# Weight pieces with both halves in one tile, the stationary ones 64 bytes behind its beginning

## The chip, the core and the metric

The kernel runs on one NeuronCore of a Trainium2 chip. The core has a matrix engine (TensorE, in the profile PE for its matmuls and PEld for its loads of the stationary operand), a vector engine (VectorE, DVE), a scalar engine (ScalarE, ACT), GpSimd (POOL) and a queue engine (SyncE, SP), which issues nearly all DMAs here. The metric is the time of one execution on the device, in microseconds (us); less is better. Matmuls write to PSUM; everything else lies in SBUF, 128 partitions wide.

A matmul has two operands in SBUF. The stationary one (128 partitions x 128 columns) is loaded into the array first, by an instruction of its own (LDWEIGHTS); the moving one (here 256 or 512 columns) is then streamed past it.

## The reference

Two layers work on x of 256 positions x 1024 features, float32. Each layer is three sublayers; each sublayer normalizes its input (RMS), computes, normalizes the result and adds it to x:

```python
for i in range(DEPTH):                     # DEPTH = 2
    h = swiglu(rms_norm(x, g[0]), w_gate[i,0], w_up[i,0], w_down[i,0]);  x = x + 0.5*rms_norm(h, g[1])
    m = dilated_attention(...) if i == 0 else retention(...);            x = x + rms_norm(m, g[3])
    h = swiglu(rms_norm(x, g[4]), w_gate[i,1], w_up[i,1], w_down[i,1]);  x = x + 0.5*rms_norm(h, g[5])
# swiglu(h) = (silu(h @ w_gate) * (h @ w_up)) @ w_down;  w_gate, w_up: 1024 x 2816, w_down: 2816 x 1024
# dilated_attention: h @ w_in (1024 x 9216: q, k, v of three groups), banded softmax, @ w_out (1024 x 1024)
# retention: h @ w_in (1024 x 8192: q, k, v, two gates), two scans, gates, @ w_out (2048 x 1024)
```

So there are four SwiGLU sublayers (FFNs), one attention and one retention, and every weight is used once.

## The kernel before

**Three products for one.** Every product of activations with weights is made of three matmuls in the type fp32r: each operand is split into a high half (a copy rounded to fp32r) and a low half (what is left), and high x high, high x low and low x high are summed in PSUM (`mm3`, L183 to 188, and the three calls of `unit_t`, L375 to 377).

**The stream of weights** (class `Stream`). A list, written down before anything runs, holds all weights in the order of use. A group is 1 MB; SP loads it into one of two `raw` buffers. A group has two pieces of [128, 1024], that is, two row blocks of 128 rows by 512 columns. `split` (L94 to 120) makes the halves of a piece: ACT writes `whi` (L109 or, where a norm's gain is multiplied in, L115, twice 512 columns), DVE then writes `wlo` (L110 or L116). `whi` and `wlo` are two tags of a pool with six buffers each, so the split runs up to six pieces ahead of the matmuls. The first pieces of a sublayer can also go to buffers that are free just then; these tiles (`wx`) hold both halves in one tile already. When the matmuls of a piece are written down, `done` calls `refill`, which writes down the split of the piece six places ahead. A `raw` buffer comes free with the split of its second piece, and the next load is issued then.

**Two ways to use a piece.** In the natural form (`piece`, `unit`, `down`: lines L186 to 188 of the profile) a block of the activations (`xh`, `xl`, `hh`, `hl` and the like, 128 columns) is stationary and 512 columns of the piece move; a piece has 2 row blocks x 2 tiles of positions x 3 = 12 such matmuls. In the transposed form (`unit_t`, L375 to 377) 128 columns of the piece are stationary and the 256 positions of `xh` or `xl` move; a piece has 2 row blocks x 4 column blocks x 3 = 24 such matmuls. For one block of columns the order is `whi` with `xh`, `whi` with `xl`, `wlo` with `xh`. An FFN has 11 units of four pieces before its down product: the first two are natural, the other nine (u = 2 to 10, `ffn_t`) transposed. In the attention the first unit and the six v units are natural, the other eleven q and k units transposed. Retention and all down products are natural.

**Places.** `xh` and `xl` have rows of 320 elements per row block (1280 bytes), and a block of 128 columns of a piece is 512 bytes, so that within their tiles all these operands begin at multiples of 256 bytes. `rows` (L383 to 393) makes a [128, 256] table, `rowsf` in an FFN, `rowsq` and `rowsk` in the attention, each in a buffer of its own; a transposed FFN unit multiplies its gate by `rowsf` (L344).

Of the kernel before, what the change touches and what calls it, by code (L numbers as in the profile page):

```python
# [6 lines left out]
F32 = mybir.dt.float32  # L7
F32R = mybir.dt.float32r
# [6 lines left out]
P = 128  # L15
# [3 lines left out]
EPS = 1e-6  # L19
NK = D // P  # L20
XC = 2 * P + 64
BIG = 1.0e30
NEWTON = -8192.0
WARM = 8
# [2 lines left out]
class Stream:  # L27


    def __init__(self, K, raw_bufs, ring):  # L30
        self.K = K
        self.raw_bufs, self.ring = raw_bufs, ring
        self.groups = []
        self.pieces = []
        self.raw = {}
        self.tiles = {}
        self.n_dma = 0
        self.n_split = 0
        self.extra = {}

    def spare(self, pieces, tags):

        self.extra.update(zip(pieces, tags))

    def add_rows(self, srcs, rows, norm):

        first = len(self.pieces)
        for k0 in range(0, rows, 4):
            g = len(self.groups)
            self.groups.append(("rows", srcs, k0))  # L50
            for j in range(2):
                k = k0 + 2 * j
                self.pieces.append((g, j, None if norm is None else norm * NK + k))
        return list(range(first, len(self.pieces)))

    def add_down(self, src, rows):

        first = len(self.pieces)
        for k0 in range(0, rows, 2):
            g = len(self.groups)  # L60
            self.groups.append(("down", src, k0))
            for j in range(2):
                self.pieces.append((g, j, None))
        return list(range(first, len(self.pieces)))
# [27 lines left out]
    def split(self):  # L92
        if self.n_split >= len(self.pieces):
            return  # L94
        i = self.n_split
        self.n_split += 1
        g, j, gain = self.pieces[i]
        while self.n_dma <= g:
            self.dma()
        nc = self.K.nc  # L100
        raw = self.raw[g][:, j * 1024 : (j + 1) * 1024]
        if i in self.extra:
            both = self.K.sb.tile([P, 2, 1024], F32R, tag=self.extra[i], name=f"wx{i}")
            hi, lo = both[:, 0], both[:, 1]
        else:
            hi = self.K.sb.tile([P, 1024], F32R, tag="whi", bufs=self.ring, name=f"whi{i}")
            lo = self.K.sb.tile([P, 1024], F32R, tag="wlo", bufs=self.ring, name=f"wlo{i}")
        if gain is None:
            nc.scalar.activation(hi, raw, AF.Copy)  # L109
            nc.vector.tensor_tensor(out=lo, in0=raw, in1=hi.bitcast(F32), op=ALU.subtract)  # L110
        else:
            for kk in range(2):
                s = slice(kk * 512, kk * 512 + 512)
                gc = self.K.gcol[:, gain + kk : gain + kk + 1]
                nc.scalar.activation(hi[:, s], raw[:, s], AF.Copy, scale=gc)  # L115
                nc.vector.scalar_tensor_tensor(  # L116
                    out=lo[:, s], in0=raw[:, s], scalar=gc, in1=hi[:, s].bitcast(F32),
                    op0=ALU.mult, op1=ALU.subtract,
                )
        self.tiles[i] = (hi, lo)  # L120
        if j == 1:
            del self.raw[g]
            while self.n_dma < len(self.groups) and self.n_dma <= g + self.raw_bufs:
                self.dma()
# [16 lines left out]
class Trunk:  # L141
# [93 lines left out]
    def pre_alloc(self, name):  # L235
        self.xh = self.sb.tile([P, NK, XC], F32R, tag="xh", name=f"xh_{name}")
        self.xl = self.sb.tile([P, NK, XC], F32R, tag="xl", name=f"xl_{name}")
        self.rstd = self.sm.tile([P, 2], F32, tag="rstd", bufs=2, name=f"rstd_{name}")
# [66 lines left out]
    def plan_ffn(self, l, i):  # L305
        wg, wu, wd = self.ffn_w_gate[l, i], self.ffn_w_up[l, i], self.ffn_w_down[l, i]
        n = l * 6 + (0 if i == 0 else 4)
        units = []
        for c in range(5):
            s = slice(c * 512, c * 512 + 512)  # L310
            units.append(self.ws.add_rows([wg[:, s]], NK, n))
            units.append(self.ws.add_rows([wu[:, s]], NK, n))
        units.append(self.ws.add_rows([wg[:, 2560:], wu[:, 2560:]], NK, n))
        return dict(units=units, down=self.ws.add_down(wd, DFF // P), l=l, n=n)

    def piece(self, j, pc, accs, ts, cols=(0, P)):
# [66 lines left out]
    def rows(self, cols, name):  # L383

        nc, sb = self.nc, self.sb
        d = sb.tile([P, 2, P], F32, tag="dg", name=f"dg_{name}")
        for t in range(2):
            nc.vector.tensor_scalar(out=d[:, t, :], in0=self.ident, scalar1=cols[:, t : t + 1], scalar2=None, op0=ALU.mult)
        tr = self.trb(f"rw_{name}")
        nc.tensor.matmul(tr[:, : 2 * P], self.ones, d, start=True, stop=True)  # L390
        r = sb.tile([P, 2 * P], F32, tag=f"rows{name}", name=f"rows{name}")
        nc.vector.tensor_copy(r, tr[:, : 2 * P])
        return r

# [152 lines left out]
    def plan_attn(self, l, j):  # L547
        units = []
        for o in range(2):
            for kind, g in (("q", 0), ("k", 0), ("q", 1), ("k", 1), ("q", 2), ("k", 2), ("v", 0), ("v", 1), ("v", 2)):  # L550
                c = g * 3072 + "qkv".index(kind) * D + o * 512
                units.append((o, kind, g, self.ws.add_rows([self.attn_w_in[j, :, c : c + 512]], NK, l * 6 + 2)))
        return dict(units=units, out=self.ws.add_down(self.attn_w_out[j], NK), l=l)

    def bias_inputs(self):
# [7 lines left out]
    def bias_table(self):  # L563
# [6 lines left out]
        rt = sb.tile([33, 48], F32, tag="E1", name="rt")  # L570
        nc.vector.memset(rt, BIG)
        nc.vector.tensor_scalar(out=rt[:32, :], in0=tr[:32, :48], scalar1=-1.0, scalar2=None, op0=ALU.mult)
# [479 lines left out]
```

## Time and profile before

| | |
|---|---|
| median of 3 runs | 1310.99 us (1310.36 to 1311.44) |
| the profiled execution | 1309.44 us |
| its span, first to last instruction | 1307.6 us, granted clock 0.997 |
| moved by DMA | 235.72 MB, mean 180 GB/s |

The profile is of one execution. It lists the busy time of each engine, the chain of work that ended last, and the groups of instructions by source line with the mean duration of one. Matmuls overlap in the pipeline, so the recorded duration of one (283 ns for 256 columns) is longer than the distance between two starts; what a matmul costs is read from how many start in a stretch of time.

### The profile page before, as it was taken

To read this page: it belongs to the slowest core of one execution; us is meant where nothing else is said; L and a number is where in the kernel's file an instruction comes from. 1 tells how busy PE (TensorE), PEld (TensorE's weight loads), DVE (VectorE), ACT (ScalarE), POOL (GpSimd) and SP (SyncE) were. 2 spreads that over 40 slices of the span, in tenths; PEclk is the share of its full clock that TensorE was granted. 3 is DMA by queue.
4 is the path that set the end of the run, shared out by engine and by line. 5 is a ranking of instruction groups with operands and counts; after the bars stand their busy time and mean duration, and the time that the engine had idled before them with its cause. 6 is when DMAs were issued, how large, how long until landed. Compare 5 with 4: busy or idle time off the path is not lost.

```text
span 1307.6 us, 20776 instructions
## 1 busy us (share of the span) xinstructions
PE 1289.3 (99%) x8362; PEld 1148.9 (88%) x8362; DVE 893.0 (68%) x1593; ACT 695.9 (53%) x1073; POOL 19.8 (2%) x17
## 2 busy tenths in 40 slices
PE   8999999999999999999999999999999999999997
PEld 6999988987998779999889998877888888899986
DVE  5766547668567768866477665589887875766644
ACT  4645445456445557854455554455555545555442
POOL 1000001000000000000000000000000000000000
PEclk9999999999999999999999999999999999999999
DMA  7655556764664346555546555645554655555551
GB/s 215 226 169 189 193 195 187 207 218 138 185 210 162 129 150 223 190 174 192 193 148 224 193 173 183 211 149 171 161 172 152 180 173 193 169 196 171 190 194 64
DMA packets 130092, 235.72 MB, mean 180 GB/s; under 512 B 25403, under 2 KB 42283, under 8 KB 129996
## 3 DMA queue, kind: packets, MB, share of 16 engines
q1 hardware_dynamic: 129852, 234.14, 56.1%
q8 instruction: 65, 1.06, 0.3%
q14 instruction: 31, 0.25, 0.1%
q10 hardware_dynamic: 144, 0.26, 0.1%
HBM read 232.21 MB, written 1.12 MB: 178 GB/s over the span
## 4 chain that ended last, share of the span: by engine, by line
PE 90%; DVE 4%; DMA 2%; ACT 2%; issue 1%; SPq 0%; DVEq 0%; ACTq 0%
PE ac_f L375 11%; PE ac_f L377 11%; PE ac_f L376 11%; PE d_f L187 6%; PE d_f L186 6%; PE d_f L188 6%; PE rt L188 4%; PE rt L187 4%; PE rt L186 4%; PE at L376 3%; PE at L377 3%; PE at L375 3%; PE at L186 2%; PE at L188 2%; PE at L187 2%; PE ac_f L186 1%
## 5 line engine op out<-in xcount | busy, mean ns | idle before, releaser
L115 ACT ACTIVATE whi<-raw,gcol 128x512 fp32r<-128x512 f32 x596 | 394.0, 715 | 321.1 <-PE ac_f L376 103.9
L116 DVE SCALAR_TENSOR_TENSOR wlo<-raw,gcol,whi 128x512 fp32r<-128x512 f32 x596 | 417.5, 748 | 157.9 <-ACT whi L115 157.1
L110 DVE TENSOR_TENSOR wlo<-raw,whi 128x1024 fp32r<-128x1024 f32 x112 | 137.2, 1225 | 136.4 <-ACT whi L109 136.1
L109 ACT ACTIVATE whi<-raw 128x1024 fp32r<-128x1024 f32 x112 | 118.8, 1061 | 169.1 <-PE d_f L188 98.5
L186 PE MATMUL d_f<-whi,hhf 128*128 128x512 f32 x352 | 137.2, 390 | 0.0
L187 PE MATMUL d_f<-wlo,hhf 128*128 128x512 f32 x352 | 137.0, 389 | 0.0
L188 PE MATMUL d_f<-whi,hlf 128*128 128x512 f32 x352 | 137.0, 389 | 0.0
L376 PE MATMUL at<-xl_f,whi 128*128 128x256 f32 x352 | 99.7, 283 | 0.0
L375 PE MATMUL at<-xh_f,whi 128*128 128x256 f32 x352 | 99.7, 284 | 0.0
L377 PE MATMUL at<-xh_f,wlo 128*128 128x256 f32 x352 | 99.6, 283 | 0.0
L186 PE MATMUL rt<-whi,xh_f 128*128 128x512 f32 x244 | 95.6, 392 | 0.2 <-ACT xh_f L232 0.2
L187 PE MATMUL rt<-wlo,xh_f 128*128 128x512 f32 x244 | 95.8, 392 | 0.0
L188 PE MATMUL rt<-whi,xl_f 128*128 128x512 f32 x244 | 95.1, 390 | 0.0
L375 PE MATMUL ac_f<-xh_in,whi 128*128 128x256 f32 x288 | 81.8, 284 | 0.0
L376 PE MATMUL ac_f<-xl_in,whi 128*128 128x256 f32 x288 | 81.6, 283 | 0.0
L377 PE MATMUL ac_f<-xh_in,wlo 128*128 128x256 f32 x288 | 81.6, 283 | 0.0
L375 PE MATMUL ac_f<-xh_at,whi 128*128 128x256 f32 x288 | 81.6, 283 | 0.0
L375 PE MATMUL ac_f<-xh_rt,whi 128*128 128x256 f32 x288 | 81.6, 283 | 0.0
L375 PE MATMUL ac_f<-xh_f,whi 128*128 128x256 f32 x288 | 81.6, 283 | 0.0
L377 PE MATMUL ac_f<-xh_at,wlo 128*128 128x256 f32 x288 | 81.5, 283 | 0.0
L377 PE MATMUL ac_f<-xh_rt,wlo 128*128 128x256 f32 x288 | 81.5, 283 | 0.0
L376 PE MATMUL ac_f<-xl_rt,whi 128*128 128x256 f32 x288 | 81.5, 283 | 0.0
(346 smaller groups left out, 2855.2 us busy)
## 6 DMA issues: line engine op xcount, KB each, us to landing
raw<-in_ffn_w_down_dram SPq DMA_DIRECT2D x44, 1024.0 KB, 4.8
raw<-in_ffn_w_up_dram SPq DMA_DIRECT2D x40, 1024.0 KB, 5.0
raw<-in_ffn_w_gate_dram SPq DMA_DIRECT2D x39, 1024.0 KB, 5.0
raw<-in_attn_w_in_dram SPq DMA_DIRECT2D x36, 1024.0 KB, 5.1
raw<-in_ret_w_in_dram SPq DMA_DIRECT2D x24, 1024.0 KB, 5.7
raw<-in_ret_w_in_dram SPq DMA_DIRECT2D x16, 512.0 KB, 3.9
raw<-in_ret_w_out_dram SPq DMA_DIRECT2D x8, 1024.0 KB, 4.8
raw<-in_ffn_w_gate_dram SPq DMA_DIRECT2D x10, 512.0 KB, 4.2
```

Of the source, the lines that this page charges most:

```text
L109: nc.scalar.activation(hi, raw, AF.Copy)
L110: nc.vector.tensor_tensor(out=lo, in0=raw, in1=hi.bitcast(F32), op=ALU.subtract)
L115: nc.scalar.activation(hi[:, s], raw[:, s], AF.Copy, scale=gc)
L116: nc.vector.scalar_tensor_tensor(out=lo[:, s], in0=raw[:, s], scalar=gc, in1=hi[:, s].bitcast(F32), op0=ALU.mult, op1=ALU.subtract,)
L186: mm(out, xh, wh, start=start, stop=False)
L187: mm(out, xh, wl, start=False, stop=False)
L188: mm(out, xl, wh, start=False, stop=stop)
L375: mm(out, hi[:, s], xh, start=k == 0 and a == 0, stop=False, skip_group_check=True)
L376: mm(out, hi[:, s], xl, start=False, stop=False, skip_group_check=True)
L377: mm(out, lo[:, s], xh, start=False, stop=k == NK - 1, skip_group_check=True)
```

## The change

The two halves of a piece become one tile `w` of 2 x 1024 + 64 elements, six buffers. A set `still` holds the pieces that will be used by `unit_t`; in these the high half begins 16 elements (64 bytes) behind the beginning of the tile and the low half right behind it; in all others at the beginning itself. The tiles of `extra` stay as they are. The ring grows from 6 x 8192 to 6 x 8448 bytes of each partition; to make room `rowsf` takes the buffer of `rowsq`.

```diff
+WC = 2 * 1024 + 64
...
-    def add_rows(self, srcs, rows, norm):
+    def add_rows(self, srcs, rows, norm, still=False):
...
+        if still:
+            self.still.update(range(first, len(self.pieces)))
...
-            hi = self.K.sb.tile([P, 1024], F32R, tag="whi", bufs=self.ring, name=f"whi{i}")
-            lo = self.K.sb.tile([P, 1024], F32R, tag="wlo", bufs=self.ring, name=f"wlo{i}")
+
+            both = self.K.sb.tile([P, WC], F32R, tag="w", bufs=self.ring, name=f"w{i}")
+            o = 16 if i in self.still else 0
+            hi, lo = (both[:, z : z + 1024] for z in (o, o + 1024))
...
-            units.append(self.ws.add_rows([wg[:, s]], NK, n))
-            units.append(self.ws.add_rows([wu[:, s]], NK, n))
-        units.append(self.ws.add_rows([wg[:, 2560:], wu[:, 2560:]], NK, n))
+            units.append(self.ws.add_rows([wg[:, s]], NK, n, c > 0))
+            units.append(self.ws.add_rows([wu[:, s]], NK, n, c > 0))
+        units.append(self.ws.add_rows([wg[:, 2560:], wu[:, 2560:]], NK, n, True))
...
-        r = sb.tile([P, 2 * P], F32, tag=f"rows{name}", name=f"rows{name}")
+        r = sb.tile([P, 2 * P], F32, tag="rowsq" if name == "f" else f"rows{name}", name=f"rows{name}")
...
-                units.append((o, kind, g, self.ws.add_rows([self.attn_w_in[j, :, c : c + 512]], NK, l * 6 + 2)))
+                units.append((o, kind, g, self.ws.add_rows([self.attn_w_in[j, :, c : c + 512]], NK, l * 6 + 2, kind != "v" and len(units) > 0)))
```

More of the change, by code (lines that the diff above doesn't have):

```diff
@@ L39, in __init__ @@
         self.extra = {}
+        self.still = set()
     def spare(self, pieces, tags):
         self.extra.update(zip(pieces, tags))
-    def add_rows(self, srcs, rows, norm):
+    def add_rows(self, srcs, rows, norm, still=False):
         first = len(self.pieces)
```

## The prediction

> **What bounds the kernel now.** The page comes first: the busy line, the slices and the chain.
>
> ```profile
> span 1307.6 us, 20776 instructions
> PE 1289.3 (99%) x8362; PEld 1148.9 (88%) x8362; DVE 893.0 (68%) x1593; ACT 695.9 (53%) x1073; POOL 19.8 (2%) x17
> ...
> PEclk9999999999999999999999999999999999999999
> ...
> PE 90%; DVE 4%; DMA 2%; ACT 2%; issue 1%; SPq 0%; DVEq 0%; ACTq 0%
> ```
>
> The matmuls are 90% of the chain and the clock is full throughout: the time is the matmul stream, and it changes only if one matmul takes another time or the stream gets gaps. A busy PE says nothing on the cost of one matmul, so the second view is the table of windows, which counts them. I laid windows over a transposed stretch (nine FFN units) and the natural stretch behind it (its down product); the first two rows count all instructions, the others those of L375 and of L186 alone, a third of the matmuls of their stretch.
>
> ```profile
> 699.00:797.00 98.00, 98.00 (x820) 98.00 (x818) 65.56 (x92) 54.25 (x83) 0.00 (x0) 1.00 0.57 189
> 607.50:666.00 58.50, 58.50 (x260) 48.39 (x259) 32.40 (x41) 28.54 (x35) 0.00 (x0) 1.00 0.60 202
> ```
> ```profile
> 699.00:797.00 98.00, 77.03 (x272) 52.17 (x272) 1.00 0.57 189
> ```
> ```profile
> 607.50:666.00 58.50, 33.47 (x86) 16.04 (x86) 1.00 0.60 202
> ```
>
> The columns are the length, then the busy time and the count of PE and PEld (and in the first two of DVE, ACT and POOL), clock, DMA share and GB/s. Transposed: 98.00 us / (3 x 272) = 120.1 ns per matmul of 256 moving columns. Natural: 58.50 / (3 x 86) = 226.7 ns per matmul of 512. So 256 more columns cost 106.6 ns, and each matmul carries a fixed 120.1 - 106.6 = 13.5 ns (from the natural row 226.7 - 213.2, the same). This fixed part is all that an address can move downwards.
>
> Is it there for any matmul with a fresh stationary operand? The plain f32 matmuls answer that: the view of their lines (duration min/median/max) and the chain, which sums eight in a row.
>
> ```profile
> L928 PEld LDWEIGHTS rqk<-ident,ro x32: 137/139/142, 881.8 to 1032.6; 128*128 128x128 f32 x32
> L928 PE MATMUL rqk<-ident,ro x32: 270/272/327, 882.0 to 1032.7; 128*128 128x128 f32 x32
> ```
> ```profile
> L938 PE MATMUL rs<-rc x32: 379/379/483, 887.6 to 1036.1; 128*128 128x256 f32 x32
> ```
> ```profile
> 929.39 0.87 PE rqk L928 x8
> ```
>
> 128 more columns cost 379 - 272 = 107 ns here (f32 streams at half the rate), and eight records of 128 columns took 0.87 us, 109 ns each: a fixed part of about 2 ns, with a load before each. So the 13.5 ns is not the price of changing the operand as such; it appears where the moving operand streams at the full rate while the next load runs.
>
> **The change part by part.** First, the address of the stationary operand. The matmuls concerned are those of L375 to 377; L375 has these groups, and the other two lines the same counts:
>
> ```profile
> L375 PE MATMUL at<-xh_f,whi 128*128 128x256 f32 x352 | 99.7, 284 | 0.0
> L375 PE MATMUL ac_f<-xh_in,whi 128*128 128x256 f32 x288 | 81.8, 284 | 0.0
> L375 PE MATMUL ac_f<-xh_at,whi 128*128 128x256 f32 x288 | 81.6, 283 | 0.0
> L375 PE MATMUL ac_f<-xh_rt,whi 128*128 128x256 f32 x288 | 81.6, 283 | 0.0
> L375 PE MATMUL ac_f<-xh_f,whi 128*128 128x256 f32 x288 | 81.6, 283 | 0.0
> ```
>
> 3 x (352 + 4 x 288) = 4512 matmuls, 4512 x 0.1201 = 542 us of the span. All have idle 0.0 before them. The next view, of one tile, shows what the addresses of before do; the load's spread is the point.
>
> ```profile
> L375 PEld LDWEIGHTS ac_f<-xh_f,whi x272: 188/192/192, 699.0 to 796.5; 128*128 128x128 f32 x136
> L375 PE MATMUL ac_f<-xh_f,whi x272: 280/283/362, 699.0 to 796.6; 128*128 128x256 f32 x136
> ```
>
> These 272 loads go through six ring buffers, eight blocks of 512 bytes each, against moving rows 1280 bytes apart: all of those are multiples of 256 bytes from the beginnings of their tiles, and all cost the same. No row of before has such a pair at an odd multiple of 64 bytes, so the price is bounded from both sides. The gain's end: the fixed part falls from 13.5 to the 2 ns of the f32 rows; 11 ns, rounded down for the two decimals of the rows, x 4512 = 49.6 us. The loss's end is under the rivals. I take the gain's end, since L928 is the nearest row in which a load runs under every matmul and costs no stall: it proves that load and stream can go side by side. That a shift of 64 bytes is what separates them here is the assumption. It has one support: the fixed part is the same for 256 and for 512 columns, so it is a stall per load of 128 columns, as two streams give that meet on the same part of the memory for the length of one load.
>
> The Trainium skill speaks against this assumption: TensorE: Matmul & The Clock Gate, section Step-by-step: what each phase is for, says that the engine has two independent read ports and that loading the next weights takes no read bandwidth from the running matmul. By that the shift changes nothing and the sum is that of the first rival. The same page's section Back-to-back issue gap gives 2.5 ns over the columns for a warm matmul alone; this trace's f32 rows agree with their 2, its fp32r rows with their 13.5 ns do not.
>
> Second, what a faster stream asks of the others. A piece lasts 24 x 0.120 = 2.88 us now and would last 24 x 0.109 = 2.62. DVE's 65.56 us and ACT's 54.25 in the 98.00 would fall into 98.00 - 816 x 0.011 = 89.0 us: 74% and 61%. The natural row already takes a piece each 12 x 0.2267 = 2.72 us at a DMA share of 0.60, and these rows show the split waiting for the matmuls, not the reverse:
>
> ```profile
> ACT whi L115 <- PE ac_f L376: 103.9, 68, 4.4
> ...
> ACT whi L109 <- PE ac_f L376: 36.1, 21, 1.8
> ```
>
> So nothing takes the gain back; if the cover went, it would first be the loads of `raw`.
>
> Third, one tile for two. `whi` came free with L376, a block's second matmul; now the buffer comes free with the `wlo` matmul, L377, so ACT's split starts up to 0.12 us (natural 0.23) later. Queued behind it on ACT are the next split and the silus and copies of the unit; DVE's `wlo` waits for it. The six pieces of the ring, 17 us of matmuls, cover it: 0. If a matmul on the high half also had to wait for DVE's write to the low half, this would show only where PE waits for a split at all:
>
> ```profile
> PE ac_f L186 <- ACT whi L115: 1.6, 1, 1.6
> ...
> PE ac_f L187 <- DVE wlo L116: 0.6, 2, 0.3
> ```
> ```profile
> L116 DVE SCALAR_TENSOR_TENSOR wlo<-raw,gcol,whi 128x512 fp32r<-128x512 f32 x596 | 417.5, 748 | 157.9 <-ACT whi L115 157.1
> ```
>
> Three places, 0.75 us each: 0 to 2.2 us. I take 0, as the halves do not overlap.
>
> Fourth, `rowsf` in the buffer of `rowsq`: in an FFN the table is written once and last read before the down product, in the attention it is written after that and last read before the next FFN. Nothing waits: 0. The natural matmuls keep both operands where they were, 0; that ACT and DVE write 64 bytes further is covered like the split itself.
>
> **Sum.** 1309.4 (the profiled execution) - 49.6 = 1259.8. That execution lies 1.6 us under the median of the runs, so the forecast is 1259.8 + 1.6 = 1261 us. Its own range is 1255 (109 ns less 107 is 1.8 unrounded, so 11.7 ns x 4512 = 52.8 us, which gives 1258, and 3 us for the rounding of the rows) to 1275 (0.7 of the gain).
>
> **Rivals.** *The fixed part stays* (no change): the 13.5 ns is fp32r's own price of a fresh operand, or 64 bytes is no step that the memory knows. For it: it is the same at every address of before and for both forms. Against: the f32 rows. 1311 us, with the third part at most 1313. That the change does not do what it says falls together with it: if the shift does not bring the two streams apart, nothing else in the change touches the stream. The skill's page SBUF — State Buffer, section Who interferes with whom, has its rule on this side, that PE and ACT never wait on anyone.
>
> *Part of the stall goes*: the two streams run at different rates, so a shift may part them for some of the load only. With half of the gain, 25 us, 1286 us; between 1275 and 1308 in all.
>
> *The load becomes longer* (slower): a block that begins 64 bytes off may touch one more unit of the memory per load. The place is the transposed stretch: PEld is busy 98.00 of 98.00 us there, against 48.39 of 58.50 in the natural one, so it decides from the first ns by which a load holds back its matmul. As price I take the difference between the loads of the two forms, 192 (above) and 188 ns:
>
> ```profile
> L187 PEld LDWEIGHTS d_f<-wlo,hhf 128*128 128x128 f32 x86 | 16.1, 188 | 3.3
> ```
>
> 4 ns x 4512 = 18 us, 1329 us. Against it: in the pipeline a load of 192 ns already fits a distance of 120.
>
> **How the numbers follow.** Forecast 0.33, part of the stall 0.22, no change 0.28, longer loads 0.17. About 0.2% (2.6 us) is what a measurement can tell from no change, so faster is 0.33 + 0.22 = 0.55, same 0.28, slower 0.17. The first three cases reach from 1255 to 1314 us and hold 0.83; beyond it lies the slower case. As both signs are open, the forecast's own range, 1255 to 1275, stands beside this one.
>
> **What would show it.** Right: the count of L375 in a transposed stretch gives about 109 ns per matmul, the nine units of an FFN last 89 us instead of 98, the natural stretch keeps its 226.7 ns, and the waits of ACT for PE shrink without vanishing. If the matmul distance falls to between 110 and 119, it was a part. Wrong: 120.1 again with an unchanged span (rival one), or over 121 with PEld still without a gap (the slower one). A distance of 109 with a span that falls by less than 45 us would mean that splits or loads have become the bound, and the PE's waits for `w` would then show up in microseconds.

## The result

The changed kernel takes 1296.03 us (median of 4 runs, 1295.72 to 1297.14) against 1311.18 for the kernel before beside it: a ratio of 0.9887, 95% interval 0.987 to 0.9904, that is 1.1% faster. Its profiled execution has a span of 1294.0 us, 13.6 less than before.

The page of the changed kernel, the lines that answer to those shown of before (its matmul lines are L381 to 383 for the transposed form and L192 to 194 for the natural one):

```profile
span 1294.0 us, 20715 instructions
PE 1276.6 (99%) x8362; PEld 1136.7 (88%) x8362; DVE 889.4 (69%) x1593; ACT 695.5 (54%) x1073; POOL 19.7 (2%) x17
...
PEclk9999999999999999999999999999999999999999
...
PE 90%; DVE 4%; ACT 2%; DMA 2%; issue 1%; SPq 0%; DVEq 0%; ACTq 0%
```

The count of matmuls, the chain's shares and the clock are the same; the stream is still the bound and has only become shorter. Where, the table of windows says. First the changed kernel, L381 alone (a third of the transposed matmuls), in the first FFN, the attention and the third FFN; the columns are as above, length first, then busy time and count of PE and PEld:

```profile
82.00:139.00 57.00, 46.31 (x168) 31.41 (x169) 1.00 0.58 186
230.00:272.00 42.00, 33.39 (x120) 22.80 (x120) 1.00 0.68 215
690.00:785.00 95.00, 75.54 (x270) 51.65 (x269) 1.00 0.59 190
```

Then the kernel before in the first FFN, and the changed kernel's natural L192 in a down product:

```profile
82.00:139.00 57.00, 44.76 (x160) 30.46 (x159) 1.00 0.55 174
```
```profile
598.50:656.50 58.00, 33.07 (x85) 15.95 (x85) 1.00 0.60 202
```

A count includes the matmul that is under way when the window begins, so a length over a count comes out up to one per cent low; starts in the timeline are the finer ruler. From one L381 (L375 before) to the third one after it are nine distances. The timeline of before in the third FFN:

```profile
699.77 0.28 PE L375 MATMUL ac_f<-xh_f,whi 128*128 128x256 f32 x1
...
700.85 0.28 PE L375 MATMUL ac_f<-xh_f,whi 128*128 128x256 f32 x1
```

That of the changed kernel, in the first and in the third FFN:

```profile
99.99 0.28 PE L381 MATMUL ac_f<-xh_in,w 128*128 128x256 f32 x1
...
101.01 0.28 PE L381 MATMUL ac_f<-xh_in,w 128*128 128x256 f32 x1
```
```profile
699.77 0.28 PE L381 MATMUL ac_f<-xh_f,w 128*128 128x256 f32 x1
...
700.83 0.28 PE L381 MATMUL ac_f<-xh_f,w 128*128 128x256 f32 x1
```

1.08 us / 9 = 120.0 ns before; 1.02 / 9 = 113.3 ns in the changed kernel's first FFN, 1.06 / 9 = 117.8 ns in its third. There are two rates, each kept without a break over hundreds of matmuls; call them the quick and the slow rhythm. Nearly all of the first FFN's nine units has the quick one (some 800 matmuls, 6.7 ns less each: 5.4 us), the other stretches nearly only the slow one (some 3700, 2.2 ns less: 8.2 us). Together 13.6 us, the whole difference of the spans. The natural down product keeps its 227 ns (58.00 / (3 x 85)).

### The profile page after: what moved, and what is told of

Same layout as the page of the kernel before. It is cut to its first block, busy times and chain, and to the rows that moved or that the text cites. A ratio compares the mean times of both kernels' runs of the same rounds, so it can differ in the third digit from the quotient of the medians.

```text
span 1294.0 us, 20715 instructions
## 1 busy us (share of the span) xinstructions
PE 1276.6 (99%) x8362; PEld 1136.7 (88%) x8362; DVE 889.4 (69%) x1593; ACT 695.5 (54%) x1073; POOL 19.7 (2%) x17
## 3 DMA queue, kind: packets, MB, share of 16 engines
q8 instruction: 65, 1.06, 0.3%
## 4 chain that ended last, share of the span: by engine, by line
PE 90%; DVE 4%; ACT 2%; DMA 2%; issue 1%; SPq 0%; DVEq 0%; ACTq 0%
PE ac_f L381 10%; PE ac_f L382 10%; PE ac_f L383 10%; PE d_f L192 6%; PE d_f L193 6%; PE d_f L194 6%; PE rt L194 4%; PE rt L193 4%; PE rt L192 4%; PE at L382 3%; PE at L383 3%; PE at L381 3%; PE at L192 2%; PE at L194 2%; DMA raw<-in_ret_w_in_dram 2%; PE at L193 2%
## 5 line engine op out<-in xcount | busy, mean ns | idle before, releaser
L121 ACT ACTIVATE w<-raw,gcol 128x512 fp32r<-128x512 f32 x596 | 394.0, 715 | 309.0 <-PE ac_f L383 101.9
L122 DVE SCALAR_TENSOR_TENSOR w<-raw,gcol,w 128x512 fp32r<-128x512 f32 x596 | 418.1, 749 | 153.9 <-ACT w L121 150.6
L116 DVE TENSOR_TENSOR w<-raw,w 128x1024 fp32r<-128x1024 f32 x112 | 137.2, 1225 | 134.5 <-ACT w L115 134.2
L115 ACT ACTIVATE w<-raw 128x1024 fp32r<-128x1024 f32 x112 | 118.8, 1061 | 166.7 <-PE d_f L194 95.7
L192 PE MATMUL d_f<-w,hhf 128*128 128x512 f32 x352 | 137.2, 390 | 0.0
L193 PE MATMUL d_f<-w,hhf 128*128 128x512 f32 x352 | 137.0, 389 | 0.0
L194 PE MATMUL d_f<-w,hlf 128*128 128x512 f32 x352 | 137.0, 389 | 0.0
L382 PE MATMUL at<-xl_f,w 128*128 128x256 f32 x352 | 99.0, 281 | 0.0
L381 PE MATMUL at<-xh_f,w 128*128 128x256 f32 x352 | 99.0, 282 | 0.0
L383 PE MATMUL at<-xh_f,w 128*128 128x256 f32 x352 | 98.9, 281 | 0.0
L192 PE MATMUL rt<-w,xh_f 128*128 128x512 f32 x244 | 95.6, 392 | 0.2 <-ACT xh_f L238 0.2
L193 PE MATMUL rt<-w,xh_f 128*128 128x512 f32 x244 | 95.8, 392 | 0.0
L381 PE MATMUL ac_f<-xh_at,w 128*128 128x256 f32 x288 | 81.0, 281 | 0.0
L381 PE MATMUL ac_f<-xh_f,w 128*128 128x256 f32 x288 | 81.0, 281 | 0.0
L381 PE MATMUL ac_f<-xh_rt,w 128*128 128x256 f32 x288 | 81.0, 281 | 0.0
L383 PE MATMUL ac_f<-xh_f,w 128*128 128x256 f32 x288 | 80.9, 281 | 0.0
L383 PE MATMUL ac_f<-xh_rt,w 128*128 128x256 f32 x288 | 80.9, 281 | 0.0
L383 PE MATMUL ac_f<-xh_at,w 128*128 128x256 f32 x288 | 80.9, 281 | 0.0
L382 PE MATMUL ac_f<-xl_at,w 128*128 128x256 f32 x288 | 80.9, 281 | 0.0
L382 PE MATMUL ac_f<-xl_f,w 128*128 128x256 f32 x288 | 80.9, 281 | 0.0
L382 PE MATMUL ac_f<-xl_rt,w 128*128 128x256 f32 x288 | 80.9, 281 | 0.0
```

The lines of the kernel that those rows point to most:

```text
L122: nc.vector.scalar_tensor_tensor(out=lo[:, s], in0=raw[:, s], scalar=gc, in1=hi[:, s].bitcast(F32), op0=ALU.mult, op1=ALU.subtract,)
L192: mm(out, xh, wh, start=start, stop=False)
L193: mm(out, xh, wl, start=False, stop=False)
L194: mm(out, xl, wh, start=False, stop=stop)
L381: mm(out, hi[:, s], xh, start=k == 0 and a == 0, stop=False, skip_group_check=True)
L382: mm(out, hi[:, s], xl, start=False, stop=False, skip_group_check=True)
```

## The experiments

**Theory** after the result: the load of the next stationary block and the moving stream hold each other up according to the distance between their addresses, and the whole settles in a steady rhythm. **Rivals**: the single tile or the other distance of the slots did it; the stationary block's own address did it; something in each stretch (data, other engines) sets its rate.

**Is it the 64 bytes?** The first four kernels change one line, the offset of the stationary pieces.

```diff
-            o = 16 if i in self.still else 0
+            o = 0            # or 8, 24, 32 elements in self.still: 32, 96, 128 bytes
```

> The changed kernel with the stationary pieces at the beginning of the tile too (offset 0), everything else as changed: one tile for both halves, slots 8448 bytes apart, rowsf in rowsq's buffer. Theory (it is the 64 bytes): 120.0 ns between the starts of the transposed matmuls in all stretches, 1311 us. Rival (it is the one tile, or the other distance of the slots): 113 and 118 ns as in the changed kernel, 1296 us.

> Stationary pieces 32 bytes behind the beginning. Theory (load and moving stream stall on each other according to their distance modulo 128 bytes, and settle in a steady rhythm): a rhythm other than 120.0, between 109 and 120 ns, 1262 to 1311 us. Rival (only steps of 64 bytes count): 120.0 ns and 1311 us.

> Stationary pieces 96 bytes behind the beginning. Theory (distance modulo 128 bytes): between 109 and 120 ns, 1262 to 1311 us, and not the same as at 32 bytes, since the load runs at half the pace of the stream. Rival (only whether the block lies on a boundary of 64 bytes, and which, counts): as at 32 bytes.

> Stationary pieces 128 bytes behind the beginning. Theory (distance modulo 128 bytes): 120.0 ns, 1311 us, as at 0. Rival (any distance from the beginning of the tile helps, or the period is longer than 128 bytes): below 120 ns, 1296 us or another time under 1308.

At 0: 1310.35 us, ratio 0.9999 (0.999 to 1.0009), the time of before. At 32 bytes 1302.18 us (0.9938, 0.9923 to 0.9953), at 96 bytes 1302.22 (0.9935, 0.992 to 0.995), at 128 bytes 1305.59 (0.9962, 0.9947 to 0.9977). Windows of L381 in the third FFN, kernels in the same order:

```profile
699.00:796.00 97.00, 76.22 (x270) 51.75 (x270) 1.00 0.59 190
```
```profile
695.00:790.00 95.00, 75.14 (x269) 50.50 (x268) 1.00 0.58 191
```
```profile
696.00:791.00 95.00, 74.93 (x268) 50.31 (x268) 1.00 0.59 190
```
```profile
697.00:793.00 96.00, 75.92 (x270) 50.81 (x270) 1.00 0.59 189
```

That is 119.8, 117.7, 118.2 and 118.5 ns by the counts; from the first start to the last in the same windows the trace gives 120.0, 118.3, 118.7 and 118.8. One window does not stand for a whole kernel: at 96 bytes the attention and most of the first FFN ran at 117.3 ns by the starts, and at 128 bytes most of the first FFN ran at 120.0. So 96 bytes equals 32 in the total, as the rival of that run had it, and not in the rates (118.3 ns throughout at 32). The one tile, the slots and `rowsf`'s new place cost and bring nothing: the first rival is out. 32 bytes count as well, so steps of 64 are not special. And 128 is not 0, by the time of the whole kernel: my expectation of a period of 128 bytes failed. (Everything in before lay at multiples of 256 bytes from the beginnings of the tiles and was alike, so a period of 256 fits.)

**The block's address or the distance?** Here the activations move too, or other pieces; `x + 64` stands for `xh` and `xl` beginning 16 elements into larger tiles.

```diff
-            o = 16 if i in self.still else 0
+            o = 48 if i in self.still else 32   # still 192 bytes, the rest 128
+            o = 16                              # all pieces 64
+            o = 0                               # x + 64
+            o = 16                              # x + 64, all pieces 64
...
-        self.xh = self.sb.tile([P, NK, XC], F32R, tag="xh", name=f"xh_{name}")
+        self.xh = self.sb.tile([P, NK * XC + 64], F32R, tag="xh", name=f"xh_{name}")[:, 16 : 16 + NK * XC].rearrange("p (k c) -> p k c", c=XC)
```

> Stationary pieces 192 bytes behind the beginning, all others (the moving ones of the natural form) 128 bytes. Theory (distance modulo 256 bytes between the block that is loaded and the stream): transposed below 120.0 ns as at every distance but 0, between 113 and 119; natural unlike 226.7 ns, at 222 to 226. Rival (the beginning of the stationary block alone counts, the place of the moving one does not): natural stays at 226.7 ns.

> All pieces 64 bytes behind the beginning, also those that move. Theory (distance): the natural matmuls whose weights lie in these tiles fall from 226.7 to 220 to 225 ns, some 2900 of them, 5 to 19 us under the changed kernel, 1277 to 1291 us. Rival (stationary address alone): as the changed kernel, 1296 us, natural 226.7 ns. A third reading (a moving operand off the boundary costs something): natural above 227 ns, over 1298 us.

> All pieces at the beginning of their tile, but xh and xl moved 64 bytes behind the beginning of theirs: they move in the transposed form and are stationary in the natural one (not in the down products). Theory (distance): transposed below 120.0 ns, 113 to 119; natural below 226.7 ns where xh and xl are stationary, unchanged in the down products. Rival (stationary address alone): transposed 120.0 ns, natural faster where xh and xl are stationary.

> xh and xl and all pieces 64 bytes behind the beginnings. Theory (distance): it is 0 again in the transposed form and in the natural one with xh and xl, so 120.0 and 226.7 ns there; the down products, with the weights at 64 and the activations at 0, as in the kernel with all pieces at 64. Rival (stationary address alone): transposed 113 to 118 ns as in the changed kernel.

1312.39 us (1.0015, 1.0005 to 1.0025), 1300.58 (0.9921, 0.9905 to 0.9937), 1303.91 (0.9952, 0.9937 to 0.9967) and 1313.91 (1.0027, 1.0016 to 1.0037). The two decisive rows are the transposed windows of the last two kernels, first with x alone moved, then with x and the pieces moved by the same 64 bytes:

```profile
694.00:784.00 90.00, 71.42 (x256) 47.87 (x255) 1.00 0.58 194
```
```profile
702.00:799.00 97.00, 76.43 (x270) 51.74 (x270) 1.00 0.56 186
```

Moving the stream instead of the block gives 117.2 ns by the count and 117.8 by the starts, the slow rhythm again; moving both gives 119.8 and 120.0, the value of before, although the stationary block lies where it lies in the changed kernel. It is the distance, not the address. Most of what this last kernel loses against before lies in the down products, whose weights moved and whose activations did not: those of the FFNs take 228.9 ns by the starts against 226.8.

The pieces at 192 bytes also ran mostly in the slow rhythm, 117.8 ns by the starts; what they gain the natural form more than loses. There the sign is the other way, and I had expected wrong: I had every distance but 0 faster. L192 in a down product, with the pieces at 192/128 and with all at 64 bytes:

```profile
607.00:664.00 57.00, 32.38 (x82) 15.35 (x82) 1.00 0.56 191
```
```profile
600.00:657.00 57.00, 32.45 (x82) 15.36 (x82) 1.00 0.57 194
```

Both 231.7 ns against 227. With x moved, the retention's natural products, which use x, change in the table of groups (mean recorded ns of one matmul; 392 before), and `d_rt`, which does not, stays:

```profile
L192 PE MATMUL rt<-w,xh_f 128*128 128x512 f32 x244 | 97.1, 399 | 0.2 <-ACT xh_f L238 0.2
...
L192 PE MATMUL d_rt<-w,zh 128*128 128x512 f32 x64 | 25.1, 392 | 0.0
```

So at 512 columns distance 0 is the best of those tried, while at 256 each distance tried up to here was faster than 0 in all or most of its stretches. With all pieces at 64 bytes the median is 1300.58 - 1296.03 = 4.6 us above the changed kernel's. That hides two things: by the starts the natural matmuls are 2.7 ns slower on average (230.0 against 227.3, some 7.5 us in all), and the attention's transposed ones ran in the quick rhythm (113.4 against 117.8, some 4.5 us less).

**More distances.** `still` becomes a table from piece to offset; each stretch has another one.

```diff
-            o = 16 if i in self.still else 0
+            o = self.still.get(i, 0)
```

> Another distance in each of the five transposed stretches: 16 bytes in the first FFN, 48 in the attention, 80 in the second, 112 in the third, 144 in the fourth FFN. Theory (the stream is held for pieces of 6.67 ns, the time of 64 bytes, by meetings with the load that depend on the distance): every stretch locks to a rhythm between 113.3 and 120.0 ns; 48 and 80 near that of 64 (113.3 or 117.8), 16 and 112 nearer to 120. Rival (multiples of 64 bytes alone differ): all five alike. If one distance gave under 113 ns in all of its stretch, a better kernel could be built with it.

> The same with 160, 176, 208, 224 and 240 bytes. Theory (period of 256 bytes): between 113.3 and 120.0 ns, 176 and 208 near 192 (mostly 117.8), 240 nearest to 120. Rival (period of 128 bytes): each as the distance 128 bytes less.

One run each, 1308.68 and 1303.47 us beside 1309.44. The windows of their transposed matmuls (L382 alone), the first kernel in the first FFN (16 bytes), the two halves of the attention (48) and the second, third and fourth FFN (80, 112, 144), then the second kernel in the second and third FFN (208, 224):

```profile
83.00:140.00 57.00, 45.04 (x161) 30.24 (x161) 1.00 0.55 176
231.00:275.00 44.00, 34.00 (x120) 22.59 (x119) 1.00 0.61 185
338.00:399.00 61.00, 48.31 (x174) 32.48 (x173) 1.00 0.66 197
511.00:606.00 95.00, 75.15 (x268) 50.30 (x267) 1.00 0.58 187
700.00:795.00 95.00, 74.74 (x264) 49.81 (x265) 1.00 0.59 188
1142.00:1237.00 95.00, 75.07 (x265) 50.16 (x264) 1.00 0.59 189
```
```profile
511.00:601.00 90.00, 71.50 (x258) 48.15 (x257) 1.00 0.59 193
697.00:787.00 90.00, 71.79 (x258) 48.34 (x258) 1.00 0.61 199
```

By the starts 118.3, then 123.3 and 117.8 in the attention, 118.8, 120.0 and 120.0; in the second kernel 116.7 and 116.7 ns. Its other stretches had 160 bytes (120.0 in the first FFN), 176 (118.1 in the attention) and 240 (120.0 in nearly all of the fourth FFN). None is under 113.3, but the theory's other end does not hold: at 48 bytes the attention's first half ran at 123.3 ns, slower than anything at distance 0, and its second half at 117.8. So distance 0 is not the worst, four other distances are no better than it, and the order cannot be told from how near a distance is to 64: 80 and 48 are equally near. A period of 128 bytes is out here too (116.7 at 208 bytes, 118.8 at 80). No distance tried removes the hold-up.

**What sets the rhythm?** A kick is one small plain f32 matmul with an unused result ahead of a transposed unit.

```diff
+        kick = self.trb("kick")
+        mm(kick[:, :P], self.ident, self.ident, start=True, stop=True)
         for j, pc in enumerate(pieces):
             hi, lo = self.ws.get(pc)
```

> The changed kernel with one small plain f32 matmul (128 moving columns, result unused) ahead of each of the 47 transposed units. Theory (two steady rhythms at this distance, 113.3 and 117.8 ns; which one a stretch gets is settled by how the stream is interrupted before it, and kept until the next interruption): within a unit one rhythm only, and units of both rhythms in stretches that had one alone. Rival (the stretch itself, its data or its neighbours on other engines, sets the rate): the first FFN stays at 113.3 and the others at 117.8 in every unit. The kicks cost some 0.3 us each, 14 us, less or more by what the rhythms give.

1300.39 us beside 1309.44, one run. L383 (its first transposed line) in four units that follow each other in the second FFN, each between two kicks:

```profile
512.70:523.10 10.40, 8.48 (x31) 5.70 (x31) 1.00 0.61 203
523.90:534.30 10.40, 8.30 (x30) 5.58 (x30) 1.00 0.58 195
535.30:545.70 10.40, 8.44 (x31) 5.75 (x31) 1.00 0.68 211
546.50:556.90 10.40, 8.30 (x30) 5.60 (x30) 1.00 0.62 209
```

Quick, slow, quick, slow: with at most one count too many, 31 and 30 in 10.40 us are the two rhythms, and the starts in the trace show 113.3 and 117.8 ns alternating from kick to kick in all five stretches, in the first FFN too: each of the 41 kicks that stand directly between two transposed matmuls turned the one rate into the other. So neither the data nor the stretch sets the rate. The interruption does: a stretch gets one of the two rhythms on entry and keeps it to the next interruption.

That suggests a better kernel: one kick where the changed kernel had the slow rhythm.

```diff
-        self.unit_t(pieces, accs)
+        self.unit_t(pieces, accs, kick=u == 3 and name != "f00")
...
-                    self.unit_t(pieces, accs)
+                    self.unit_t(pieces, accs, kick=u in (2, 10))
```

> The changed kernel with five kicks in all (one small plain f32 matmul each, result unused): ahead of unit 3 in the second, third and fourth FFN, ahead of the second and of the second o-half's second transposed unit in the attention, behind the last interruption of each of these stretches, where the changed kernel ran at 117.8 ns. Theory (a kick turns one rhythm into the other, and it then stays): 113.3 ns from each kick to the end of its stretch, 3 x 768 + 384 + 480 = 3168 matmuls x 4.4 ns = 14 us, less 5 x 0.23 us for the kicks: 1283 us. Rival (the alternation in the kernel with a kick per unit came from something that goes with the units): still 117.8 ns in whole or in part, 1296 to 1298 us.

1287.82 us (median of 5, 1285.37 to 1290.74), ratio 0.9829 (0.9812 to 0.9846): 1.7% faster than before and the best of all. Windows of its L384 in the second, third and fourth FFN and the two halves of the attention, and the timeline at one kick:

```profile
510.00:594.00 84.00, 68.32 (x248) 46.40 (x247) 1.00 0.61 201
695.00:779.00 84.00, 68.29 (x247) 46.40 (x248) 1.00 0.59 196
1133.00:1217.00 84.00, 68.32 (x248) 46.40 (x247) 1.00 0.57 189
231.00:270.00 39.00, 31.07 (x111) 21.25 (x111) 1.00 0.59 190
342.00:394.00 52.00, 42.29 (x154) 28.72 (x154) 1.00 0.63 202
```
```profile
508.12 0.28 PE L386 MATMUL ac_f<-xh_at,w 128*128 128x256 f32 x1
508.24 0.39 PE L373 MATMUL kick<-ident 128*128 128x128 f32 x2
508.38 0.37 PE L384 MATMUL ac_f<-xh_at,w 128*128 128x256 f32 x1
508.59 0.28 PE L385 MATMUL ac_f<-xl_at,w 128*128 128x256 f32 x1
```

Four of five kicks did what was expected: 84.00 / (3 x 248) = 112.9 and 52.00 / (3 x 154) = 112.6 ns by the counts, 113.3 by the starts, to the end of each stretch. The fourth row is the miss: 39.00 / (3 x 111) = 117.1 ns. In this execution the attention's first half was in the quick rhythm already, and the kick turned it into the slow one. The changed kernel's profile had entered the same place in the slow rhythm, with the same instructions ahead of it. So what a stretch gets on entry is not the same in these two executions. Of the 5 us by which the forecast of 1283 us missed, this explains by the starts some 1.7 us here and 0.7 us in the first FFN, which was partly in the slow rhythm; another 1.7 us is that the first transposed matmul started later (39.48 us against 37.80). The rest, and whether the entry is also behind the 5 us over which the runs spread, one profile cannot tell.

## Why the prediction was wrong

The direction and the place held, and the wide range from 1255 to 1314 us, in which no change lies as well; the forecast's own range, 1255 to 1275, and its size did not: 49.6 us were forecast and 15 came. The step that failed is the price in the first part: "I take the gain's end, since L928 is the nearest row in which a load runs under every matmul and costs no stall". That price was 11 ns per matmul. Of the 13.3 ns over the columns (120.0 - 106.7) the change removes 6.7 in the quick rhythm and 2.2 in the slow one, on average 13.6 us / 4512 = 3.0 ns. The f32 row was near in its load but not in its stream, which by the prediction's own rows runs at half the rate; that this is why it shows no such fixed part is likely and not shown, since no run moved an f32 operand. The one support named there was none: the 213.2 ns are twice the difference between the two rows, so the natural row gives back the fixed part of the transposed one whatever that is. It says nothing on a stall per load. The rival "part of the stall goes" (1275 to 1308 us, chance 0.22) is what happened. Its reason, that a shift parts the two streams for some of the load only, fits and is not shown. (A slip on which nothing hangs: 0.7 of the gain gives 1276 us as the range's end, not 1275.)

Point by point. That the fixed part depends on where the two operands lie: shown, by moving either and both. That it is a stall per load: argued, no run shows what waits for what. That it is the same for all the multiples of 256 bytes in the kernel: right, 120.0 ns throughout. I did not ask whether the same shift would help the natural form; it hurts there. The one tile, `rowsf` and the split's later start at 0: right, by the kernel with offset 0 (0.9999). The cover of the other engines: right; the splits still wait for the matmuls, in the changed kernel's view of waits

```profile
ACT w L121 <- PE ac_f L383: 101.9, 75, 4.3
```

against 103.9 us before. "No change" is out by its interval. The slower rival, a longer load, is out too, and its row points the other way: the loads became shorter. The groups of the changed kernel in the first FFN's window and in the third's:

```profile
L381 PEld LDWEIGHTS ac_f<-xh_in,w 128*128 128x128 f32 x169 | 31.7, 188 | 0.0
```
```profile
L381 PEld LDWEIGHTS ac_f<-xh_f,w 128*128 128x128 f32 x269 | 51.6, 192 | 0.0
L382 PEld LDWEIGHTS ac_f<-xl_f,w 128*128 128x128 f32 x270 | 50.7, 188 | 0.0
L383 PEld LDWEIGHTS ac_f<-xh_f,w 128*128 128x128 f32 x269 | 50.5, 188 | 0.0
```

Before, the median of the transposed loads was 192 ns. In the quick rhythm they take 188, in the slow one two of three do. I had read that 4 ns as a cost that might grow. It is no measure of the stall either: the natural loads take 188 ns, and their matmuls carry the fixed part all the same.

The Trainium skill's rule that was weighed against the forecast (TensorE: Matmul & The Clock Gate, section Step-by-step: what each phase is for: loading the next weights takes no read bandwidth from the running matmul) does not hold for this stream. By it the shift would have changed nothing; with both operands moved alike a matmul takes 120 ns, with one moved 118 or 113. Whether it is read bandwidth that the two share, no run shows.

What stays open: why there are two rhythms, and what on entry chooses between them. The rates fit a stall in portions of 6.67 ns, the time of 16 columns or 64 bytes of the stream: 120.0, 117.8 and 113.3 ns are 106.7 and 6, 5 and 3 such portions per three matmuls. That is a fit to these three and not shown; 116.7 and 118.3 ns at other distances would be 4.5 and 5.25 portions, so it is not the whole rule, and nothing here gives the order of the distances.

## What to carry to other kernels

Where the matrix engine is the bound and each matmul carries a fixed part beyond its columns, look at the distance between the stationary block and the moving operand in SBUF: 64 bytes were worth 1.1% here, and only a trial of each form tells which distance is good: the same shift helped 256 columns and hurt 512, and 48 bytes could be worse than none. Measure the distance between starts per stretch, not the mean over the kernel: two stretches with the same instructions ran at different rates. As the upper end of a gain, take a row that is like the changed instruction in both its streams.

## What the runs showed of the hardware that was not expected

- A stream of equal fp32r matmuls of 256 columns has, at a distance of 64 bytes, two steady rates, 113.3 and 117.8 ns; in no profile did a stretch at this distance change its rate without an interruption, its first ten matmuls aside. Other distances have two rates as well: 117.3 and 118.7 ns at 96 bytes, 118.7 and 120.0 at 128, 117.8 and 123.3 at 48.
- One f32 matmul of 128 columns in between turned the one rate into the other, from unit to unit over all five stretches, at some 0.23 us each; where the quick rate followed it paid for itself within about 50 matmuls.
- The rate that a stretch gets on entry differs between two executions whose instructions are the same up to there: from 44 us on the first FFN ran at 113.3 ns in the changed kernel's profile, and at 117.8 ns up to 66 us in that of the kernel with five kicks. Each kernel has one profile, so two executions of one kernel were not compared.
- At distance 0 all is steady: 120.0 ns and 226.7 ns at every multiple of 256 bytes and in every stretch.
